# Turning two chunks of scaled keys with one 128x128 transpose, and 32-token products on the column quarters for the second mixer's diagonal and short block lengths

## The chip, the cores and the metric

One core of one Trainium2 chip runs one inference step of a small recurrent decoder. The metric is the time of one execution on the device, in microseconds; lower is better. All arithmetic is in 32-bit floats. TensorE has two lanes in the profile: PE (the matmuls) and PEld (the loads of the stationary operand, which overlap them). A matmul on plain f32 operands leaves two records, since it runs in two passes; one on operands of type fp32r leaves one.

## The reference

Two layers over 512 prompt tokens and 8 samples of 4 tokens (544 columns in all). Layer 0 runs two recurrent mixers side by side (RG-LRU and RWKV-7), layer 1 one (HGRN2), each followed by a gated feed-forward block. Of these, two places matter here. In RWKV-7 a 64x64 matrix state per head is updated by every token:

```python
S = (S * w_t[:, :, None, :] - sk[..., None] * (kk_t * a_t)[:, :, None, :]
     + v_t[..., None] * k_t[:, :, None, :])
return S, jnp.einsum('bhvk,bhk->bhv', S, r_t)
```

In HGRN2 token t attends to every earlier token s with a weight that holds, per channel, the product of all decays between them:

```python
diff = bc[:, :, :, None, :] - bc[:, :, None, :, :]
dec = jnp.exp(jnp.where(mask, diff, -jnp.inf))
att = jnp.einsum('bhtsk,bhtk,bhsk->bhts', dec, qc, kc)
```

## The kernel before

Everything is held with channels on the 128 partitions and the 544 tokens along the free axis. The dense layers are 128x128 weight tiles against 272-token halves. Each weight is split into a high and a low fp32r part (`wh` on ScalarE, `wl` on VectorE or GpSimd, L210 and L213), and three products per tile (high by high, high by low, low by high) accumulate in PSUM tiles named `acc`. Nearly all matmuls are issued through one helper, `mm`, so they carry the line L179; they are told apart by their tiles.

**First mixer (`mixer0`).** RWKV-7 runs in chunks of 64 tokens, two heads on the 128 partitions, four pairs p of heads. Four things are prepared before the scan over chunks. `scores` makes masked products. `keys(p, w)` (L708 to L728) scales the keys by the decay of their chunk (`KH`, on GpSimd, in two buffers) and turns them so that tokens stand on the partitions (`TM`): `turn` multiplies each 64x64 block by an identity, two per chunk and sixteen per call into one PSUM tile `tmps`, and one ScalarE copy of 128x512 takes that to `TM`. A 64-column piece for the samples (`KHs`, L723) is turned behind it when w is 1. A triangular inverse in 32x32 blocks is made by a chain of VectorE steps, `Pd` and `Y` (L683, L685), which starts when `Ns` has been gathered from DRAM and ends in a store (`y_p`) and sixteen loads of the tile `T` (L698). `join` (tiles `jps`) puts the blocks together with 32x32 matmuls. The string `MID` gives the order of these pieces. From the piece `r3` on, the order of TensorE is the order of the code; that of the other engines is set by a scheduler.

**Second mixer (`mixer1`).** HGRN2 works head by head (8 heads) in `mix`. The 512 prompt tokens are four chunks of 128. The attention matrix `A` of a chunk (tokens s on the partitions, t along the free axis) is built from a diagonal and seven levels with block lengths b = 1, 2, 4, ... 64. Before level b, `K` and `Q` have been multiplied by the decays within blocks of b tokens (GpSimd for `K`, L1567; VectorE for `Q`, L1568), so that their plain product is right exactly where s stands in an even block and t in the odd block behind it. Each level multiplies 64 tokens s by the 64 tokens t of the chunk's odd blocks, eight 64x64 products (`lv`) for the four chunks and two halves, though only the pairs in neighbouring blocks are wanted; `copy_predicated` with the mask `lmask` takes these to `A` (L1570). The 32 sample tokens ride along: one 32x32 product `d0s`, and one 32x16 product each at b = 1 and 2. At b = 64 there are four products, one per chunk, copied by ScalarE (L1575). The diagonal (`d0`, in the trace's names `d`) is eight 64x64 products masked by an identity (L1549). In this stage TensorE also runs in the order of the code: behind each level, `fill(FILL[l])` issues 27, 13, 13, 24, 10, 23 and 5 matmuls of the next head's projections, during which `K` and `Q` are brought to the next level.

Of the kernel before, what the change touches and what calls it, by code (L numbers as in the profile page):

```python
# [11 lines left out]
F32 = mybir.dt.float32  # L12
F32R = mybir.dt.float32r
I32 = mybir.dt.int32
# [16 lines left out]
CH = 64  # L31
# [54 lines left out]
def consts_np():  # L86
# [42 lines left out]
    for l in range(7):  # L129
        b = 1 << l  # L130
        t = np.array([x for x in range(128) if (x // b) % 2])[None, :]
        lv.append(((s // b) + 1 == t // b).astype(np.int32))
    c["lmask"] = np.stack(lv, 1)
    return {k: np.ascontiguousarray(v) for k, v in c.items()}


class Build:
# [205 lines left out]
    def mixer0(self):  # L343
# [359 lines left out]
        def turn(out, src):  # L703
            for par in range(2):
                r = par_rows[par]
                self.mm(out[r], src[r], ident[r, r])

        def keys(p, w):  # L708
# [7 lines left out]
            yield  # L716
            ps = self.ms.tile([128, NCH, CH], F32, tag="m", name="tmps")
            for c in range(NCH):
                turn(ps[:, c], KH[:, c])
            ACT(TM[p][:, w], ps, AF.Copy)  # L720
            if w:
# [695 lines left out]
    def mixer1(self, xg):  # L1417
# [5 lines left out]
        p = self.open("m1")  # L1423
        lmask = p.tile([128, 7, 64], I32, name="lmask")
        nc.sync.dma_start(lmask, I["lmask"])
# [5 lines left out]
        for i in range(2):  # L1431
            nc.gpsimd.memset(Am[i][64:128, :, 0:64], 0.0)
        qms = [p.tile([128, NB, 32], F32, name=f"qm{i}") for i in range(2)]
# [20 lines left out]
        def tmp(name, shape=None, bufs=2):  # L1454
            return p.tile(shape or [128, NT], F32, tag=name, name=name, bufs=bufs)

        def blk(z, b, n):
            return z[:, 0:n].rearrange("p (m g b) -> p m g b", g=2, b=b)
# [77 lines left out]
        def mix(h, late):  # L1536
# [4 lines left out]
            As = tmp("As", [32, 32])  # L1541
            ps = self.ms.tile([128, 4, 64], F32, tag="m", name="d0")
            for c in range(4):
                for g in range(2):
                    ks = slice(128 * c + 64 * g, 128 * c + 64 * g + 64)
                    self.mm(ps[64 * g:64 * g + 64, c], K[:, ks], q0[:, ks])
            for g in range(2):
                r = slice(64 * g, 64 * g + 64)
                TT(A[r, :, r], ps[r], self.ident[r, None, r].to_broadcast([64, 4, 64]), OP.mult)  # L1549
            ps = self.ms.tile([32, 32], F32, tag="m", name="d0s")  # L1550
            self.mm(ps, K[:, SEQ:], q0[:, SEQ:])
            TT(As, ps, self.ident[0:32, 0:32], OP.mult)
            for l in range(7):
                b = 1 << l
                ps = self.ms.tile([128, 5, 64], F32, tag="m", name="lv")
                for c in range(4):
                    for g in range(2 if b < 64 else 1):
                        ks = slice(128 * c + 64 * g, 128 * c + 64 * g + 64)
                        self.mm(ps[64 * g:64 * g + 64, c], K[:, ks],
                                blk(Q[:, 128 * c:128 * c + 128], b, 128)[:, :, 1])  # L1560
                if b <= 2:
# [6 lines left out]
                TT(qv[:, :, 1], qv[:, :, 1], g2[:, :, 0, None].to_broadcast([128, m, b]), OP.mult)  # L1568
                if b < 64:
                    nc.vector.copy_predicated(  # L1570
                        A.rearrange("p c (m g b) -> p c m g b", g=2, b=b)[:, :, :, 1],
                        lmask[:, l, None, :].to_broadcast([128, 4, 64]).rearrange("p c (m b) -> p c m b", b=b),
                        ps[:, 0:4].rearrange("p c (m b) -> p c m b", b=b))
                else:
                    ACT(A[0:64, :, 64:], ps[0:64, 0:4], AF.Copy)  # L1575
                if b <= 2:
                    nc.vector.copy_predicated(
                        blk(As, b, 32)[:, :, 1], lmask[0:32, l, 0:16].rearrange("p (m b) -> p m b", b=b),
                        ps[0:32, 4, 0:16].rearrange("p (m b) -> p m b", b=b))
# [198 lines left out]
```

## Time and profile before

| | |
|---|---|
| median of 3 runs | 1546.02 us (1541.61, 1546.02, 1546.65) |
| the profiled execution | 1542.56 us, span 1540.8 us, mean granted clock 0.981 |
| PE busy | 1480.7 us of the span |
| VectorE (DVE) busy | 831.7 us |
| ScalarE (ACT) busy | 549.4 us |
| GpSimd (POOL) busy | 401.9 us |
| `mixer1`, from the first `d0` product to the last level | 809 to 1060 us of the span |
| first turned keys to the last | 106 to 168 us of the span |

A row of the timeline gives the start, the length, the engine, the line, the operation with its tiles and its shape, and how many instructions were merged; brackets give the idle time before it and what ended it. The length of a merged row runs from the first start to the last end, so the last instruction's own duration is in it. A shape such as 128\*64 128x64 means that 128 rows and 64 columns of the array were used and that the moving operand had 128 partitions and 64 elements.

### The profile page before, as it was taken

To read this page: it belongs to the slowest core of one execution; us is meant where nothing else is said; L and a number is where in the kernel's file an instruction comes from. 1 tells how busy PE (TensorE), PEld (TensorE's weight loads), DVE (VectorE), ACT (ScalarE), POOL (GpSimd) and SP (SyncE) were. 2 spreads that over 40 slices of the span, in tenths; PEclk is the share of its full clock that TensorE was granted. 3 is DMA by queue.
4 is the path that set the end of the run, shared out by engine and by line. 5 is a ranking of instruction groups with operands and counts; after the bars stand their busy time and mean duration, and the time that the engine had idled before them with its cause. 6 is when DMAs were issued, how large, how long until landed. Compare 5 with 4: busy or idle time off the path is not lost.

```text
span 1540.8 us, 34923 instructions
## 1 busy us (share of the span) xinstructions
PE 1480.7 (96%) x14688; PEld 1432.2 (93%) x14688; DVE 831.7 (54%) x1542; ACT 549.4 (36%) x983; POOL 401.9 (26%) x520
## 2 busy tenths in 40 slices
PE   7988899879999999999999999999999999999998
PEld 6877898669999999999999999999999999999997
DVE  6776346655544444434576666666674433443444
ACT  4642144453432233223352333333453322232224
POOL 3583245422110011001123434444431100110010
PEclk9999999879999999999999999999999999999999
DMA  4222221132232322322231222322333223223221
GB/s 159 70 71 85 59 80 41 43 97 76 83 90 89 87 92 83 91 88 88 82 121 63 86 95 85 104 92 87 101 122 92 90 83 90 90 90 90 84 75 59
DMA packets 87405, 132.89 MB, mean 86 GB/s; under 512 B 24368, under 2 KB 30384, under 8 KB 87120
## 3 DMA queue, kind: packets, MB, share of 16 engines
q1 hardware_dynamic: 87248, 130.66, 27.4%
q8 instruction: 115, 1.88, 0.5%
q14 instruction: 42, 0.34, 0.1%
HBM read 120.13 MB, written 10.50 MB: 85 GB/s over the span
## 4 chain that ended last, share of the span: by engine, by line
PE 85%; DVE 6%; ACT 3%; DMA 2%; issue 2%; POOL 1%; SPq 1%; DVEq 0%; ACTq 0%; POOLq 0%
PE acc L179 74%; PE lv L179 2%; PE ops L179 2%; PE ch L179 1%; PE jps L179 1%; SPq L698 1%; DMA wf<-w_out_ab 1%; PE ds L179 0%; PE tr L1593 0%; PE nps L179 0%; DVE Y L685 0%; DVE wl L213 0%; ACT wh L210 0%; DMA wd<-down 0%; PE opsm L179 0%
## 5 line engine op out<-in xcount | busy, mean ns | idle before, releaser
L179 PE MATMUL acc<-xg,wh 128*128 128x272 f32 x4544 | 877.2, 291 | 12.6 <-ACT xg L270 6.2
L179 PEld LDWEIGHTS acc<-xg,wh 128*128 128x128 f32 x4544 | 717.1, 190 | 20.5 <-ACT xg L270 6.5
L179 PE MATMUL acc<-xg,wl 128*128 128x272 f32 x2272 | 651.6, 292 | 0.1
L210 ACT ACTIVATE wh<-wf 128x512 fp32r<-128x512 f32 (+1 forms) x404 | 250.9, 621 | 630.2 <-PE acc L179 521.8
L179 PEld LDWEIGHTS acc<-xg,wl 128*128 128x128 f32 x2272 | 427.0, 190 | 4.5 <-issue 0.8
L213 DVE TENSOR_TENSOR wl<-wf,wh 128x512 fp32r<-128x512 f32 (+1 forms) x373 | 267.2, 717 | 188.9 <-ACT wh L210 163.0
L1297 POOL TENSOR_TENSOR S<-S,rstd 128x272 f32<-128x272 f32 x88 | 74.7, 849 | 645.5 <-ACT S L1296 645.4
L179 PE MATMUL acc<-h,wh 128*128 128x272 f32 x1280 | 236.9, 288 | 0.0
L179 PEld LDWEIGHTS acc<-h,wh 128*128 128x128 f32 x1280 | 198.0, 188 | 0.0
L179 PE MATMUL acc<-h,wl 128*128 128x272 f32 x640 | 176.7, 287 | 0.0
L179 PEld LDWEIGHTS acc<-h,wl 128*128 128x128 f32 x640 | 118.1, 188 | 0.0
L1300 DVE TENSOR_TENSOR hh<-acc,S 128x272 f32<-128x272 f32 x88 | 38.9, 441 | 126.2 <-PE acc L179 124.7
L179 PE MATMUL acc<-cat,wh 128*128 128x272 f32 (+2 forms) x512 | 99.5, 294 | 7.3 <-ACT wh L210 7.3
L179 PEld LDWEIGHTS acc<-cat,wh 128*128 128x128 f32 x512 | 81.8, 192 | 8.2 <-ACT wh L210 7.8
L1296 ACT ACTIVATE S<-t 128x272 f32<-128x272 f32 x88 | 37.8, 431 | 122.2 <-DVE t L1295 122.2
L1317 DVE TENSOR_TENSOR x<-acc,x 128x272 f32<-128x272 f32 x80 | 35.0, 439 | 81.3 <-PE acc L179 81.0
L179 PE MATMUL acc<-cat,wl 128*128 128x272 f32 (+2 forms) x256 | 73.6, 295 | 3.4 <-POOL wl L213 3.1
L1295 DVE TENSOR_TENSOR t<-acc,rstd 128x272 f32<-128x272 f32 x88 | 38.7, 441 | 70.1 <-PE acc L179 70.1
L288 POOL TENSOR_TENSOR ssq<-ssq,sq 128x544 f32<-128x544 f32 x33 | 46.6, 1411 | 87.6 <-ACT sq L287 84.9
L1567 POOL TENSOR_TENSOR K<-K,G 128x256 f32<-128x256 f32 (+1 forms) x48 | 39.2, 817 | 78.5 <-PE lv L179 78.5
L213 POOL TENSOR_TENSOR wl<-wf,wh 128x512 fp32r<-128x512 f32 x31 | 41.5, 1343 | 65.7 <-ACT wh L210 65.5
L179 PEld LDWEIGHTS acc<-cat,wl 128*128 128x128 f32 x256 | 48.6, 192 | 4.4 <-POOL wl L213 3.6
(368 smaller groups left out, 1560.0 us busy)
## 6 DMA issues: line engine op xcount, KB each, us to landing
wf<-gate SPq DMA_DIRECT2D x88, 256.0 KB, 2.7
wf<-up SPq DMA_DIRECT2D x88, 256.0 KB, 2.8
wf<-down SPq DMA_DIRECT2D x72, 256.0 KB, 2.7
wf<-w_in_c SPq DMA_DIRECT2D x64, 256.0 KB, 2.6
wf<-w_in_ab SPq DMA_DIRECT2D x44, 256.0 KB, 2.8
x<-xT SPq DMA_DIRECT2D x16, 272.0 KB, 4.8
wf<-w_out_ab SPq DMA_DIRECT2D x16, 256.0 KB, 2.6
S<-hS SPq DMA_DIRECT2D x8, 512.0 KB, 3.6
```

Of the source, the lines that this page charges most:

```text
L179: return self.seq(self.nc.tensor.matmul(out, lhsT, rhs, start=start, stop=stop, skip_group_check=True), chain)
L210: nc.scalar.activation(wh[:, :n], wf[:, :n], AF.Copy)
L213: eng.tensor_tensor(wl[:, :n], wf[:, :n], wh[:, :n].bitcast(F32), OP.subtract)
L288: eng.tensor_tensor(self.ssq, self.ssq, t, OP.add)
L698: nc.sync.dma_start(T[quarter(par, half), :, p, CB * half:CB * half + CB], y_p[2 * p + par, half::2].rearrange("c i t -> i c t"))
L1295: nc.vector.tensor_tensor(t[:, c], ps, rs()[:, c], OP.mult)
L1296: nc.scalar.activation(S[:, c], t[:, c], AF.Silu)
L1297: nc.gpsimd.tensor_tensor(S[:, c], S[:, c], rs()[:, c], OP.mult)
L1300: nc.vector.tensor_tensor(hh[:, c], ps, S[:, c], OP.mult)
L1317: nc.vector.tensor_tensor(x[:, c], ps, x[:, c], OP.add)
L1567: PTT(kv[:, :, 0], kv[:, :, 0], g2[:, :, 1, None].to_broadcast([128, m, b]), OP.mult)
```

## The change

Three edits. First, `keys` turns two chunks at a time: a block of 128 partitions (two heads) by 128 tokens (two chunks) goes through one transpose, four per call instead of sixteen products; since its result has the tokens of the two chunks on the two halves of the partitions and the heads along the free axis, four ScalarE copies of 64 partitions by 256 elements sort it into `TM`. Second, the diagonal and the levels b = 1 to 16 of `mixer1` use products of 32 tokens s, at the four 32-column groups of the array and so on the four 32-partition quarters of PSUM: sixteen products with 32 columns for the diagonal, sixteen with the 16 odd-block tokens of the same quarter for a level. They land in a compact tile `Ad` (128 by 4 by 32); at b = 16 four GpSimd copies spread it into `A`. Third, b = 32 is eight 32x32 products (quarter 0 against 1, quarter 2 against 3), copied by two ScalarE instructions. The mask shrinks, and `A` is now zeroed whole.

```diff
-            ps = self.ms.tile([128, NCH, CH], F32, tag="m", name="tmps")
-            for c in range(NCH):
-                turn(ps[:, c], KH[:, c])
-            ACT(TM[p][:, w], ps, AF.Copy)
+            ps = self.ms.tile([128, 4, 128], F32, tag="m", name="tmps")
+            for c in range(4):
+                self.seq(nc.tensor.transpose(ps[:, c], KH[:, 2 * c:2 * c + 2].rearrange("p c t -> p (c t)"), ident))
+            for odd in range(2):
+                for par in range(2):
+                    ACT(TM[p][par_rows[par], w, odd::2], ps[par_rows[odd], :, par_rows[par]], AF.Copy)
...
-            nc.gpsimd.memset(Am[i][64:128, :, 0:64], 0.0)
+            nc.gpsimd.memset(Am[i], 0.0)
...
-            ps = self.ms.tile([128, 4, 64], F32, tag="m", name="d0")
+            quads = [slice(32 * q, 32 * q + 32) for q in range(4)]
+            ps = self.ms.tile([128, 4, 32], F32, tag="m", name="d0")
             for c in range(4):
-                for g in range(2):
-                    ks = slice(128 * c + 64 * g, 128 * c + 64 * g + 64)
-                    self.mm(ps[64 * g:64 * g + 64, c], K[:, ks], q0[:, ks])
-            for g in range(2):
-                r = slice(64 * g, 64 * g + 64)
-                TT(A[r, :, r], ps[r], self.ident[r, None, r].to_broadcast([64, 4, 64]), OP.mult)
+                for r in quads:
+                    ks = slice(128 * c + r.start, 128 * c + r.stop)
+                    self.mm(ps[r, c], K[:, ks], q0[:, ks])
+            Ad = tmp("Ad", [128, 4, 32])
+            TT(Ad, ps, sum4[:, None, :].to_broadcast([128, 4, 32]), OP.mult)
...
                 for c in range(4):
-                    for g in range(2 if b < 64 else 1):
-                        ks = slice(128 * c + 64 * g, 128 * c + 64 * g + 64)
-                        self.mm(ps[64 * g:64 * g + 64, c], K[:, ks],
-                                blk(Q[:, 128 * c:128 * c + 128], b, 128)[:, :, 1])
+                    Kc, Qc = K[:, 128 * c:128 * c + 128], Q[:, 128 * c:128 * c + 128]
+                    if b < 32:
+                        for r in quads:
+                            self.mm(ps[r, c, 0:16], Kc[:, r], blk(Qc[:, r], b, 32)[:, :, 1])
+                    elif b == 32:
+                        for r, t in ((quads[0], quads[1]), (quads[2], quads[3])):
+                            self.mm(ps[r, c, 0:32], Kc[:, r], Qc[:, t])
+                    else:
+                        self.mm(ps[0:64, c], Kc[:, 0:64], Qc[:, 64:128])
...
-                if b < 64:
+                if b < 32:
                     nc.vector.copy_predicated(
-                        A.rearrange("p c (m g b) -> p c m g b", g=2, b=b)[:, :, :, 1],
-                        lmask[:, l, None, :].to_broadcast([128, 4, 64]).rearrange("p c (m b) -> p c m b", b=b),
-                        ps[:, 0:4].rearrange("p c (m b) -> p c m b", b=b))
+                        Ad.rearrange("p c (m g b) -> p c m g b", g=2, b=b)[:, :, :, 1],
+                        lmask[:, l, None, :].to_broadcast([128, 4, 16]).rearrange("p c (m b) -> p c m b", b=b),
+                        ps[:, 0:4, 0:16].rearrange("p c (m b) -> p c m b", b=b))
+                elif b == 32:
+                    for r, t in ((quads[0], quads[1]), (quads[2], quads[3])):
+                        ACT(A[r, :, t], ps[r, 0:4, 0:32], AF.Copy)
                 else:
                     ACT(A[0:64, :, 64:], ps[0:64, 0:4], AF.Copy)
+                if b == 16:
+                    for r in quads:
+                        nc.gpsimd.tensor_copy(A[r, :, r], Ad[r])
```

On TensorE nothing changes its place; only the counts and shapes of these products do. At the start of a head in `mixer1` the program of before has these rows on that engine (`d` is the diagonal, `d0s` the samples' product, `lv` level b = 1, `acc` the projections that fill):

```order
L179 MATMUL d_10039<-q_9958,K 64x64 x8
L179 MATMUL d0s<-q_9958,K 32x32
L179 MATMUL lv<-Q,K 64x64 x8
L179 MATMUL lv<-Q,K 32x16
L179 MATMUL acc<-xg,wh 128x272 x2
```

The changed program has these at the same place:

```order
L179 MATMUL d_9967<-q_9886,K 32x32 x16
L179 MATMUL d0s<-q_9886,K 32x32
L179 MATMUL lv<-Q,K 32x16 x17
L179 MATMUL acc<-xg,wh 128x272 x2
L179 MATMUL acc<-xg,wl 128x272
```

Sixteen smaller products stand for eight, and the samples' 32x16 product now has the shape of its neighbours.

On GpSimd, from the `K` update of b = 16 to that of b = 64 in the first head, before (`G` are decay products of the next head's projection):

```order
L1567 TENSOR_TENSOR K<-K,G 128x16x16
L1493 TENSOR_TENSOR G<-G 128x8
L1493 TENSOR_TENSOR G<-G 128x4
L1567 TENSOR_TENSOR K<-K,G 128x8x32
L1567 TENSOR_TENSOR K<-K,G 128x4x64
```

and in the changed program:

```order
L1574 TENSOR_TENSOR K<-K,G 128x16x16
L1495 TENSOR_TENSOR G<-G 128x16
L1588 COPY A_9708<-Ad 32x4x32 x4
L1495 TENSOR_TENSOR G<-G 128x8
L1574 TENSOR_TENSOR K<-K,G 128x8x32
L1495 TENSOR_TENSOR G<-G 128x4
L1574 TENSOR_TENSOR K<-K,G 128x4x64
```

The four copies, which wait for VectorE's last masked copy into `Ad`, stand ahead of the `K` update of b = 32.

In `mixer0` the scheduler moves GpSimd's work around the second pair of keys (`KH` and `KHs` are the scaled keys, `d` the difference of neighbouring tokens for the next projection, `Ws` a piece of the scores' input):

```order
 L487 TENSOR_TENSOR d<-X 128x544
-L710 TENSOR_TENSOR KH<-KB_248,ebT 128x512
-L488 TENSOR_TENSOR d<-shift,X 128x8
-L710 TENSOR_TENSOR KH<-KB_248,ebT 128x512
+L710 TENSOR_TENSOR KH<-KB_248,ebT 128x512 x2
 L713 TENSOR_TENSOR KHs<-KBs_260,ebT 128x64
-L745 TENSOR_TENSOR Ws_254<-rm,eb_292 64x32
-L745 TENSOR_TENSOR Ws_258<-rm,eb_292 64x32
-L478 MEMSET X 128x1
+L488 TENSOR_TENSOR d<-shift,X 128x8
 L710 TENSOR_TENSOR KH<-KB_249,ebT 128x512
```

The small `d` of L488 now stands behind both scalings and `KHs` instead of between them, and a third scaling comes ahead of `Ws`.

More of the change, by code (lines that the diff above doesn't have):

```diff
@@ L132, in consts_np @@
         lv.append(((s // b) + 1 == t // b).astype(np.int32))
-    c["lmask"] = np.stack(lv, 1)
+    c["lmask"] = np.ascontiguousarray(np.tile(np.stack(lv, 1)[0:32, 0:5, 0:16], (4, 1, 1)))
     return {k: np.ascontiguousarray(v) for k, v in c.items()}
@@ L1423, in mixer1 @@
         p = self.open("m1")
-        lmask = p.tile([128, 7, 64], I32, name="lmask")
+        lmask = p.tile([128, 5, 16], I32, name="lmask")
         nc.sync.dma_start(lmask, I["lmask"])
```

## The prediction

> **What bounds the kernel now.** I read the page's totals first, then the shares of the chain of waits, then the windows of the two stages that the change touches.
>
> ```profile
> span 1540.8 us, 34923 instructions
> PE 1480.7 (96%) x14688; PEld 1432.2 (93%) x14688; DVE 831.7 (54%) x1542; ACT 549.4 (36%) x983; POOL 401.9 (26%) x520
> PE 85%; DVE 6%; ACT 3%; DMA 2%; issue 2%; POOL 1%; SPq 1%; DVEq 0%; ACTq 0%; POOLq 0%
> ```
>
> TensorE is busy in 96% of the span and holds 85% of the chain that ended last; no other engine comes near. Next the stretch of `mixer1` in which the diagonals and levels lie, and one of `mixer0` (per engine: busy us and instructions; then granted clock and DMA).
>
> ```profile
> core 0: us, PE busy (x) PEld busy (x) DVE busy (x) ACT busy (x) POOL busy (x), PEclk, DMA share, GB/s
> 800.00:1070.00 270.00, 269.89 (x2817) 251.31 (x2815) 185.87 (x370) 91.18 (x180) 113.93 (x147) 1.00 0.26 85
> 140.00:150.00 10.00, 7.88 (x303) 6.85 (x300) 4.39 (x11) 1.20 (x2) 0.65 (x4) 0.83 0.43 110
> ```
>
> In `mixer1` TensorE has no gap (269.89 of 270.00) at full clock, and its order is that of the code, so time taken from its products there comes off the end one for one while nothing else is late. In `mixer0` it has gaps, and there the chain has to be read step by step.
>
> **The change, part one: the diagonal and the levels in `mixer1`.** These rows are the second and third head's, from product to the filling `acc` behind it. A plain f32 product leaves two records.
>
> ```profile
> 869.13 0.69 PE L179 MATMUL d<-q,K 128*64 128x64 f32 x16
> 869.92 0.85 PE L179 MATMUL lv<-Q,K 128*64 128x64 f32 x18
> 870.71 0.51 PE L179 MATMUL acc<-xg,wh 128*128 128x272 f32 x2
> 844.24 0.85 PE L179 MATMUL lv<-Q,K 128*64 128x64 f32 x18
> 845.03 0.52 PE L179 MATMUL acc<-xg,wh 128*128 128x272 f32 x2
> 846.85 0.69 PE L179 MATMUL lv<-Q,K 128*64 128x64 f32 x16
> 847.47 0.39 PE L179 MATMUL acc<-xg,wh 128*128 128x272 f32 x1
> 855.17 0.69 PE L179 MATMUL lv<-Q,K 128*64 128x64 f32 x16
> 855.79 0.52 PE L179 MATMUL acc<-xg,wh 128*128 128x272 f32 x2
> ```
>
> From start to the next `acc`, the diagonal with `d0s` and b = 1 takes 870.71 - 869.13 = 1.58 us, b = 2 takes 0.79, b = 4 takes 0.62 (8 and 16 have its shape), b = 32 takes 0.62. Per head that is 1.58 + 0.79 + 3 x 0.62 + 0.62 = 4.85 us. The four products of b = 64 stay.
>
> No row before shows a full-height product of 32 columns with 16 moving elements. The nearest are these: 32x32 tiles with 16 moving elements on four places of the array (`jp`, `jz`), with 32 elements on two places (`jg`, `ja`), and full-height products of 32 columns in four column groups, but with 128 moving elements (`opsq`).
>
> ```profile
> 150.34 1.26 PE L179 MATMUL jps<-jp,jz 32*32 32x16 f32 x128
> 151.53 0.52 PE L179 MATMUL acc<-xg,wh 128*128 128x272 f32 x2
> L179 PE MATMUL jps<-jp,jz 32*32 32x16 f32 x256 | 2.5, 180 | 0.0
> 168.91 1.38 PE L179 MATMUL jps<-jg,ja 32*32 32x32 f32 x64
> 836.43 0.65 PE L179 MATMUL opsq<-S,qm 128*32 128x128 f32 x16
> L179 PE MATMUL opsq<-S,qm 128*32 128x128 f32 x128 | 5.2, 279 | 0.0
> ```
>
> Taking the last record's own duration out, the spacing is (1.26 - 0.18)/127 = 8.5 ns for the first, (1.38 - 0.2)/63 = 18.7 ns for the second (its 0.2 is my estimate, after the first's 180 ns), and (0.65 - 0.279)/15 = 24.7 ns for the third. From the last record's start to the `acc` behind it, 151.53 - (151.60 - 0.18) = 0.11 us pass. I take 8.5 ns for the products on four quarters: the last row shows that four column groups of full height do run side by side (four records of 279 ns in 4 x 24.7 = 99 ns), and its stream is eight times as long as the new one, so the price lies toward the row that shares the length of 16. For b = 32, on two quarters only, I take 18.7. Both ends, 8.5 and 24.7, stay for the range.
>
> - Diagonal, `d0s`, b = 1: 68 records, 67 x 8.5 + 0.11 and 0.05 for the samples' products, which have no neighbour to share the array with: 0.73, so -0.85 us.
> - b = 2: 34 records, 33 x 8.5 + 0.11 = 0.39, so -0.40.
> - b = 4, 8, 16: 32 records, 31 x 8.5 + 0.11 = 0.37, so -0.25 each, -0.75.
> - b = 32: 16 records, 15 x 18.7 + 0.11 = 0.39, so -0.23.
>
> That is 2.23 us a head, and **17.8 us for eight heads**. It all goes to the time if the updates between levels stay covered. Each level's update of `K` and `Q` begins when the level ends and has the filling products beside it, whose number does not change; a shorter level moves both alike.
>
> What is new there stands on GpSimd and ScalarE. Four copies, 32 partitions by 128 elements, follow VectorE's last masked copy at b = 16.
>
> ```profile
> L1004 POOL COPY am<-Ws 64x32 f32<-64x32 f32 x16 | 3.8, 238 | 10.5 <-PE opss L179 5.8 <-PE rpss L179 4.2
> L617 POOL COPY Ws<-kap 64x8 f32<-64x8 f32 x8 | 3.4, 429 | 0.3
> 853.88 0.88 POOL L1567 TENSOR_TENSOR K<-K,G 128x256 f32<-128x256 f32 x1 [0.34 <-PE lv L179]
> 855.95 0.67 POOL L1567 TENSOR_TENSOR K<-K,G 128x256 f32<-128x256 f32 x1 [0.75 <-PE lv L179]
> 858.85 0.68 PE L179 MATMUL lv<-Q,K 128*64 128x64 f32 x8
> L1575 ACT ACTIVATE A<-lv 64x256 f32<-64x256 f32 x8 | 3.0, 378 | 9.7 <-PE lv L179 9.7
> ```
>
> GpSimd copies cost 238 to 429 ns here, so four are 1.0 to 1.7 us. The order puts them behind the `K` update that ends at 853.88 + 0.88 = 854.76, with one `G` product of about 0.24 between, and ahead of the update that b = 64 waits for: that would end by 854.76 + 0.24 + 1.7 + 0.67 = 857.4 at the latest. b = 64 starts at 858.85, less 0.23 of its own head's b = 32: 858.6. About 1.2 us is left, so I count them at nothing; if that cover went, each us would cost 8 us in all. ScalarE's two copies at b = 32 (378 ns or less each) feed nothing until the end of the head. VectorE's masked copies shrink from 256 elements to 64; that engine is not late there. The smaller mask and the whole memset come once, ahead of the stage: nothing.
>
> **Part two: the turned keys in `mixer0`.** Rows for a 128x128 transpose and for sixteen products by the identity (32 records), then steps of the chain of waits:
>
> ```profile
> 860.42 0.60 PE L1593 MATMUL tr<-ident,V 128*128 128x128 f32 x4
> 860.85 0.60 PE L1593 MATMUL tr<-ident,K 128*128 128x128 f32 x4
> 135.99 1.15 PE L179 MATMUL tmps<-ident,KH 64*64 64x64 f32 x32
> 143.52 1.90 DMA T<-y_p
> 163.78 0.55 PE tmps L179 x13
> 164.32 1.72 issue
> 166.04 0.80 PE tmps L179 x19
> 166.87 0.60 ACT L720 ACTIVATE TM<-tmps 128x512 f32<-128x512 f32 x1 [2.68 <-PE tmps L179]
> ```
>
> Four transposes take 860.85 - 860.42 = 0.43 us against 1.15 (1.35 without the stall for the last call, 0.55 + 0.80). There are eight calls; those before 143 lie in front of the wait for the loads of `T`, which end at 143.52 + 1.90 = 145.42, and win nothing. Only the last call's stand on the chain: 0.43 - 1.35 = -0.9 us, with the 1.72 of `issue`, whose cause no row names, left in. ScalarE makes four copies for one; at most four times 0.60 instead of 0.60, with 2.68 us idle ahead of it. Only a consumer straight behind the last call would see 1.8 us of that.
>
> Against this stands the order. `d` of L488 moves behind `KH` and `KHs`, and VectorE's `rm` waits for it:
>
> ```profile
> 109.40 0.22 POOL L488 TENSOR_TENSOR d<-shift,X 128x8 f32<-128x8 f32 x1
> 109.66 0.78 DVE L489 SCALAR_TENSOR_TENSOR rm<-d,vec,X 128x544 f32<-128x544 f32 x1 [4.34 <-POOL d L488]
> 110.04 1.30 POOL L710 TENSOR_TENSOR KH<-KB,ebT 128x512 f32<-128x512 f32 x1 [0.42 <-PE tmps L179]
> 111.30 0.74 POOL L713 TENSOR_TENSOR KHs<-KBs,ebT 128x64 f32<-128x64 f32 x1
> ```
>
> `rm` comes later by up to 1.30 + 0.74 - 0.42 = 1.6 us. VectorE's queue then holds the triangular chain, which ends in the store and loads of `T`; since `rm` comes once ahead of that chain, and VectorE has waited 4.34 us for it, I put about half, +0.7, on the loads of `T`. Together **-0.2 us**, with bounds of -3 (-0.9 and the whole stall of 1.72 gone with the burst, `rm` hidden: -2.6) and +3 (`rm` and the ScalarE copies whole, 1.6 + 1.8 - 0.9 = 2.5).
>
> **Sum.** On the profiled execution: 1542.56 - 17.8 - 0.2 = 1524.6 us. The median of the runs, 1546.02, lies 3.46 above that execution, which gives 1528.0 on its basis. I predict 1528.
>
> **The rivals.** A measurement of this kernel tells about 0.3%, 4.6 us, from no change.
>
> *The small products cannot start faster than the full-height row shows.* Then 24.7 ns holds for all 67 + 33 + 93 + 15 = 208 intervals of a head: 208 x 24.7 + 0.71 (the tails) = 5.85 us against 4.85, so +1.0 a head and +8.0 in all: 1550.4 on the profile's basis, 1554 on the median's, slower. It decides from (4.85 - 0.71)/208 = 19.9 ns up. For it: the only full-height row has 24.7, and the record count of a level doubles. Against it: that row's stream is long, and `jp`, `jz` shows 8.5 from the same queue with as many weight loads. The Trainium skill ("TensorE: Matmul & The Clock Gate", section "Wait — 56ns, not 53.3ns?") says that start-to-start never drops below about 25 ns however small the product, which is this rival; the 8.5 ns of tiles that share the array contradict it for 32 rows, and no run here shows it for 128 rows. "Instruction Overhead" in the Trainium skill's "TensorEngine Tiling (Array Packing)" warns against tiling a dimension that is already small, on the same ground.
>
> *Only two of the four column groups run together*, as the row at 18.7 ns: 208 x 18.7 + 0.71 = 4.60, -0.25 a head, -2.0 in all: 1540.4, or 1543.8 on the median's basis; no change that can be told. `opsq` speaks against it.
>
> *GpSimd's copies hold b = 64 back.* If a copy took 0.7 us or more, 2.8 for four, the 1.2 us left would be overrun by a little; at 0.95 each by about 1 us a head, and the time would be 1536. Their price of 429 ns for 8 elements speaks for caution.
>
> *`mixer0` gives back its upper bound*: +3 instead of -0.2, 1531.
>
> **How the numbers follow.** The forecast with `mixer0` anywhere in its bounds has 0.78; the copies 0.08; two groups 0.08; the 25 ns floor 0.06. The first two are faster by over 0.3%, the third is the same, the last slower: 0.86, 0.08, 0.06. The forecast's own bounds are 1528 - 3 - some 3 for a mean spacing of 7 ns (208 x 1.5 ns x 8 = 2.5), 1521, and upward 1531 to 1536 by the two rivals that stay faster; 1540 leaves out the third and the last.
>
> **What would show it.** In the profile after, `lv` rows of 32 records with the next `acc` 0.37 us behind their start, and 0.73 from the first `d` to `acc`; rows at 0.9 would be the floor. TensorE still without a gap from 800 on, and no wait for `K` or a copy ahead of b = 64. In `mixer0`, four transposes in 0.43 us, the end of `T`'s loads against 145.42, and the stall near 164. The prediction is wrong if the spacing lies above 12 ns, or if TensorE waits anywhere in `mixer1`.

## The result, and the profile after

| | before | changed |
|---|---|---|
| median of 4 runs | 1545.05 us | 1523.46 us (1521.26 to 1527.63) |
| ratio | | 0.9866, 95% interval 0.9838 to 0.9894 |
| profiled execution | 1542.56 us, span 1540.8 | 1527.63 us, span 1525.6 |

The change makes the kernel faster by 21.6 us on the medians; 1528 was predicted, with its bounds at 1521 and 1540. The profiled execution is the longest of the four, so stages are compared below, not spans.

First the totals and the chain of waits of the changed kernel, as on the page:

```profile
span 1525.6 us, 36071 instructions
PE 1466.0 (96%) x15232; PEld 1419.6 (93%) x15232; DVE 807.9 (53%) x1526; ACT 561.1 (37%) x1023; POOL 415.7 (27%) x552
PE 86%; DVE 5%; issue 3%; ACT 2%; POOL 2%; DMA 2%; SPq 0%; DVEq 0%; POOLq 0%; ACTq 0%
```

TensorE has 544 more records and 14.7 us less busy time, and still bounds the kernel. The windows of the two stages:

```profile
core 0: us, PE busy (x) PEld busy (x) DVE busy (x) ACT busy (x) POOL busy (x), PEclk, DMA share, GB/s
800.00:1070.00 270.00, 269.59 (x3712) 253.91 (x3711) 174.00 (x369) 104.15 (x212) 133.82 (x183) 1.00 0.27 93
140.00:150.00 10.00, 7.77 (x210) 5.89 (x210) 2.76 (x6) 0.00 (x0) 0.57 (x3) 0.63 0.37 74
150.00:160.00 10.00, 8.54 (x208) 7.51 (x209) 2.20 (x5) 1.95 (x4) 0.00 (x0) 0.69 0.08 29
```

`mixer1` has stayed without a gap worth counting. In `mixer0`, at the joins, the granted clock is lower than before (0.63 against 0.83 at 140 to 150).

**Where the time went.** The rows of one tile give the first and last start of its instructions. From the first head's diagonal `d` to the last `opsm`, which forms the last head's output, the kernel before and then the changed one:

```profile
L179 PE MATMUL d<-q,K x128: 222/222/270, 809.1 to 1039.2; 128*64 128x64 f32 x128
L179 PE MATMUL opsm<-sum,Oi x16: 276/286/297, 838.5 to 1070.3; 128*128 128x32 f32 x16
L179 PE MATMUL d<-q,K x256: 195/196/218, 810.7 to 1026.2; 128*32 128x32 f32 x128
L179 PE MATMUL opsm<-sum,Oi x16: 275/286/298, 838.0 to 1055.2; 128*128 128x32 f32 x16
```

That stage took 1070.3 - 809.1 = 261.2 us and takes 1055.2 - 810.7 = 244.5: 16.7 us less, 2.09 a head. What follows it is the same to 0.1 us (1540.8 - 1070.3 = 470.5, 1525.6 - 1055.2 = 470.4). What precedes it ends 1.6 us later in these two executions, though the medians say the opposite: 21.6 - 16.7 = 4.9 us must be won there. So the runs below are read by two numbers each: this stage, from the profile, and the rest ahead of it, the median less the time from the first `d` to the end of the span (before: 1545.05 - 731.7 = 813.4; changed: 1523.46 - 714.9 = 808.6; 2 us outside of the span are in it).

The levels of the second head after the change, from products to the `acc` behind them:

```profile
838.39 0.46 PE L179 MATMUL d<-q,K 128*32 128x32 f32 x32
839.15 0.51 PE L179 MATMUL acc<-xg,wh 128*128 128x272 f32 x2
842.94 0.49 PE L179 MATMUL lv<-Q,K 128*32 128x16 f32 x34
843.36 0.52 PE L179 MATMUL acc<-xg,wh 128*128 128x272 f32 x2
845.19 0.45 PE L179 MATMUL lv<-Q,K 128*32 128x16 f32 x32
845.56 0.39 PE L179 MATMUL acc<-xg,wh 128*128 128x272 f32 x1
852.79 0.45 PE L179 MATMUL lv<-Q,K 128*32 128x32 f32 x16
853.16 0.52 PE L179 MATMUL acc<-xg,wh 128*128 128x272 f32 x2
```

Diagonal to b = 1 takes 0.76 us (0.73 was predicted), b = 2 takes 0.42 (0.39), b = 4 takes 0.37 (0.37), b = 32 takes 0.37 (0.39).

### The profile page after: what moved, and what is told of

It is laid out like the page before. It is cut to its first block, busy times and chain, and to the rows that moved or that the text cites. A ratio compares the mean times of both kernels' runs of the same rounds, so it can differ in the third digit from the quotient of the medians.

```text
span 1525.6 us, 36071 instructions
## 1 busy us (share of the span) xinstructions
PE 1466.0 (96%) x15232; PEld 1419.6 (93%) x15232; DVE 807.9 (53%) x1526; ACT 561.1 (37%) x1023; POOL 415.7 (27%) x552
## 3 DMA queue, kind: packets, MB, share of 16 engines
q8 instruction: 119, 1.95, 0.5%
## 4 chain that ended last, share of the span: by engine, by line
PE 86%; DVE 5%; issue 3%; ACT 2%; POOL 2%; DMA 2%; SPq 0%; DVEq 0%; POOLq 0%; ACTq 0%
PE acc L179 77%; PE ops L179 2%; PE lv L179 2%; PE ch L179 1%; DMA wf<-w_out_ab 1%; PE nps L179 1%; POOL wl L213 1%; PE jps L179 0%; PE ds L179 0%; PE tr L1606 0%; POOL KH L710 0%; PE opsm L179 0%; PE gps L179 0%; PE rpss L179 0%; ACT wh L210 0%
```

## The experiments

All times in one table; each kernel was timed beside the kernel before on its chip. "Stage" and "ahead" are the two numbers explained above. "Turned" says which keys go through the 128x128 transpose.

| kernel | turned | median, us | ratio to before, interval | stage | ahead |
|---|---|---|---|---|---|
| before | none | 1545.05 | | 261.2 | 813.4 |
| the change | all | 1523.46 | 0.9866, 0.9838 to 0.9894 | 244.5 | 808.6 |
| levels_only | none | 1530.63 | 0.9906, 0.9887 to 0.9925 | 244.4 | 815.6 |
| keys_only | all | 1543.28 | 0.9986, 0.9973 to 1.0000 | 261.2 | 811.3 |
| change_again | all | 1521.87 | 0.9859, 0.9837 to 0.9881 | 244.5 | 806.9 |
| four_groups | all | 1520.61 | 0.9850, 0.9830 to 0.9871 | 241.7 | 808.7 |
| by_quarter | all | 1542.77 | 0.9986, 0.9974 to 0.9998 | 263.3 | 809.2 |
| half_stream | none | 1543.80 | 0.9993, 0.9975 to 1.0010 | 260.2 | 813.4 |
| copies_8 (and a shorter group norm) | all | 1529.10 | 0.9892, 0.9876 to 0.9908 | 247.7 | 811.1 |
| keep_warm | all | 1523.26 | 0.9855, 0.9838 to 0.9871 | 244.4 | 808.1 |
| last_keys | last pair | 1524.34 | 0.9851, 0.9830 to 0.9872 | 244.4 | 809.7 |
| first_keys | all but last pair | 1523.73 | 0.9856, 0.9834 to 0.9879 | 244.5 | 807.9 |
| pad_j | all | 1519.34 | 0.9839, 0.9820 to 0.9858 | 241.9 | 807.3 |
| best | last pair | 1522.94 | 0.9851, 0.9831 to 0.9871 | 241.8 | 810.3 |

The stage repeats to 0.2 us wherever the levels are the same; "ahead" carries all the scatter.

The granted clock is a good part of why. In all fourteen traces it is either 1.0 or 0.5, and every stretch at 0.5 lies in the first 362 us or in the last 9, none in the stage. To take this out I multiplied each run's span by its mean granted clock, which is on record for every run. That is an estimate of the time at full clock, and it flatters a kernel whose clock is low while TensorE waits anyway. Over the 52 runs of the kernel before, the span and the part of it lost to the clock (span times one less the clock) go together with a correlation of 0.70, which is half of the scatter; the mean at full clock is 1512.2 us.

### The two halves of the change apart

`levels_only` keeps the second and third edit and turns keys as before:

```diff
+            ps = self.ms.tile([128, NCH, CH], F32, tag="m", name="tmps")
+            for c in range(NCH):
+                turn(ps[:, c], KH[:, c])
+            ACT(TM[p][:, w], ps, AF.Copy)
```

> The diagonal and levels of the change, with the keys turned as before. Theory 1 (the levels carry the gain): from the first diagonal product to the last output sum of mixer1 the stage is 14.6 us shorter over seven heads as in the profile of the change (2.09 a head), so about 16.7 us below the kernel before, ratio near 0.989. Theory 2 (the turned keys carry part of the measured 21.6 us): this kernel stays 3 to 6 us behind the whole change.

`keys_only` is the kernel before with the first edit alone (the lines of `keys` in the diff above).

> Only the turned keys, the second mixer as before. Theory 1: within 3 us of the kernel before, with rm and so the loads of T about 2 us later, as in the profile of the change, and 0.9 us won at the last call. Theory 2 (the keys carry part of the gain): 3 to 6 us faster than before.

`change_again` is the change, unaltered.

> The change itself once more beside its parts. If the parts add up, its gain is that of the levels alone plus that of the keys alone to within 2 us. Theory 1: 16 to 18 us below before; theory 2: 20 to 22.

The stage falls by 16.8 us with the levels alone and by nothing with the keys alone, so that half is settled. In the runs, the levels alone win 0.94% (14.5 us, interval 11.6 to 17.5) and the keys alone 0.14% (2.2 us, 0 to 4.2); the whole wins 1.41% (21.8 us) on the same chip. The last is 5 us more than the sum of the parts (14.5 + 2.2), which the intervals only just allow. Of theory 2's figures only that of the whole came out (20 to 22): the levels alone stay 7 to 9 us behind the whole change by the medians, not 3 to 6, and the keys alone win less than 3. At full clock, by the estimate above, the parts do add: on that chip the means of the runs fall by 17.7 us with the levels, 7.0 with the keys and 25.4 with both.

### Why a small product is cheap

`by_quarter` issues the same products quarter by quarter, so that neighbours in the queue share a column group:

```diff
-            for c in range(4):
-                for r in quads:
+            for r in quads:
+                for c in range(4):
...
+                if b < 32:
+                    for r in quads:
+                        for c in range(4):
+                            Kc, Qc = K[:, 128 * c:128 * c + 128], Q[:, 128 * c:128 * c + 128]
+                            self.mm(ps[r, c, 0:16], Kc[:, r], blk(Qc[:, r], b, 32)[:, :, 1])
...
-                        for r in quads:
-                            self.mm(ps[r, c, 0:16], Kc[:, r], blk(Qc[:, r], b, 32)[:, :, 1])
+                        pass
```

> The change with the diagonal and b = 1 to 16 issued quarter by quarter (four chunks of one column group behind each other) instead of chunk by chunk. Same products, same count. If the gain comes from four column groups that work side by side, neighbours in the queue now share a group and run one behind the other: a level of 32 records takes 0.8 to 1.0 us instead of 0.37, about +3 us a head, 20 to 28 us in all. If the products are only limited by how fast they can be issued (about 8 ns a record), nothing changes.

Its timeline, level b = 4 of the second head:

```profile
844.72 0.89 PE L179 MATMUL lv<-Q,K 128*32 128x16 f32 x32
845.54 0.39 PE L179 MATMUL acc<-xg,wh 128*128 128x272 f32 x1
```

The level takes 0.82 us instead of 0.37 and the stage 263.3 us instead of 244.5, 18.8 more (20 to 28 were expected); with that the second mixer is slower than before the change. Same products, same count, another order. The spacing is (0.82 - 0.11)/31 = 22.9 ns within a group, and (0.37 - 0.11)/31 = 8.4 ns over four. A quarter of 22.9 would be 5.7, so over four groups something else sets the pace, and no run shows what. The floor that the Trainium skill states ("TensorE: Matmul & The Clock Gate", section "Wait — 56ns, not 53.3ns?", start-to-start never below about 25 ns) is thus about right here for one column group, by these 22.9 ns, and not for products that alternate between four.

`half_stream` keeps 64-token products in two groups and halves only what streams through them:

```diff
-                        self.mm(ps[64 * g:64 * g + 64, c], K[:, ks],
-                                blk(Q[:, 128 * c:128 * c + 128], b, 128)[:, :, 1])
+                        if b < 64:
+                            self.mm(ps[64 * g:64 * g + 64, c, 32 * g:32 * g + 32], K[:, ks],
+                                    blk(Q[:, ks], b, 64)[:, :, 1])
+                        else:
+                            self.mm(ps[0:64, c], K[:, ks], Q[:, 128 * c + 64:128 * c + 128])
...
+                    for g in range(2):
+                        r, s = slice(64 * g, 64 * g + 64), slice(32 * g, 32 * g + 32)
+                        nc.vector.copy_predicated(
+                            A[r, :, r].rearrange("p c (m g b) -> p c m g b", g=2, b=b)[:, :, :, 1],
+                            lmask[r, l, None, s].to_broadcast([64, 4, 32]).rearrange("p c (m b) -> p c m b", b=b),
+                            ps[r, 0:4, s].rearrange("p c (m b) -> p c m b", b=b))
```

> The kernel before (64-token products, two column groups), but each level below 64 multiplies only by the 32 odd-block tokens of its own 64-token half, and VectorE copies each half apart. Keys as before. If a product's streaming time in its group sets the pace, a level falls to 16 records at about 15 ns, 0.35 us, as in the change with its 32 records, and the levels win about 1.3 us a head, 10 to 11 us in all, without any quarter. If the four quarters are what wins, a level stays at 0.5 us or more and the gain is under 6 us.

Its level b = 4:

```profile
848.83 0.66 PE L179 MATMUL lv<-Q,K 128*64 128x32 f32 x16
849.42 0.39 PE L179 MATMUL acc<-xg,wh 128*128 128x272 f32 x1
```

0.59 us against 0.62 before: half the stream wins 0.03 us, and 1.0 us in the whole stage. The first theory is wrong for products of 64 columns. With the last record's own duration taken out (0.22 us in its group, 0.20 in that of `d`), a record takes (0.66 - 0.22)/15 = 29 ns with 64 columns and 32 moving elements; the diagonal of the change, also with 32 moving elements but 32 columns, takes (0.46 - 0.20)/31 = 8.4 ns. So at the same stream the price depends on the columns of a product and the number of groups in turn. That half the stream wins next to nothing here is in line with the Trainium skill's "TensorEngine Tiling (Array Packing)", section "Instruction Overhead", that a product with one moving element takes as long as one with 60; its warning against tiling what is small already does not hold here, since the four groups overlap.

A long stream does count: over the same four groups a record of 32 columns takes 24.7 ns with 128 elements (`opsq`), and 8.4 with 32 or with 16.

`four_groups` takes the same thought further. Odd chunks of b = 32 land one quarter higher and odd chunks of b = 64 on the upper half:

```diff
-                        for r, t in ((quads[0], quads[1]), (quads[2], quads[3])):
-                            self.mm(ps[r, c, 0:32], Kc[:, r], Qc[:, t])
+                        for q in (0, 2):
+                            self.mm(ps[quads[q + c % 2], c, 0:32], Kc[:, quads[q]], Qc[:, quads[q + 1]])
                     else:
-                        self.mm(ps[0:64, c], Kc[:, 0:64], Qc[:, 64:128])
+                        self.mm(ps[64 * (c % 2):64 * (c % 2) + 64, c], Kc[:, 0:64], Qc[:, 64:128])
...
+                    for q in (0, 2):
+                        for z in range(2):
+                            ACT(A[quads[q], z::2, quads[q + 1]], ps[quads[q + z], z:4:2, 0:32], AF.Copy)
...
+                    for z in range(2):
+                        ACT(A[0:64, z::2, 64:], ps[64 * z:64 * z + 64, z:4:2], AF.Copy)
```

> The change, with b = 32 spread over all four column groups (odd chunks land one quarter higher) and b = 64 over two halves, six ScalarE copies instead of three. If spacing is set by how many column groups work side by side: b = 32 falls from about 0.39 to 0.25 us and b = 64 from about 0.6 to 0.37, 0.3 to 0.4 us a head and 2.5 to 3 us in all below the change. If a floor per product or the weight loads set it: no difference.

Its second head, b = 32 and b = 64:

```profile
852.40 0.33 PE L179 MATMUL lv<-Q,K 128*32 128x32 f32 x16
852.66 0.52 PE L179 MATMUL acc<-xg,wh 128*128 128x272 f32 x2
855.72 0.45 PE L179 MATMUL lv<-Q,K 128*64 128x64 f32 x8
856.10 0.39 PE L179 MATMUL acc<-xg,wl 128*128 128x272 f32 x1
```

b = 32 takes 0.26 us (0.37 in the change) and b = 64 takes 0.38 (0.61 in the change). The stage is 2.8 us shorter, as expected of groups that work side by side.

### The cover on GpSimd

`copies_8` makes each copy of the diagonal block twice. It differs in a second place, which its expectation does not name: the group norm of `mixer0` makes two refinement steps instead of three, three small VectorE instructions fewer each time. That lies ahead of the stage, so only the stage of this kernel is read, and not its time:

```diff
-            for _ in range(3):
+            for _ in range(2):
                 TT(w, y, y, OP.mult)
...
                     for r in quads:
-                        nc.gpsimd.tensor_copy(A[r, :, r], Ad[r])
+                        for _ in range(2):
+                            nc.gpsimd.tensor_copy(A[r, :, r], Ad[r])
```

> The change with each GpSimd copy of the diagonal block made twice, eight instead of four a head. In the profile of the change the four took 1.82 us and the K update behind them ended at 855.20, 1.02 us ahead of b = 64. If that slack is all the cover there is, 1.8 us more overruns it by 0.8 us a head: +6 us, with TensorE waiting for K ahead of b = 64. If GpSimd is far off the path: no change.

The change's GpSimd in the second head, and TensorE's b = 64:

```profile
852.51 1.82 POOL L1588 COPY A<-Ad 32x128 f32<-32x128 f32 x4
854.58 0.62 POOL L1574 TENSOR_TENSOR K<-K,G 128x256 f32<-128x256 f32 x1
856.22 0.68 PE L179 MATMUL lv<-Q,K 128*64 128x64 f32 x8
```

`K` is ready at 854.58 + 0.62 = 855.20, 1.02 us ahead of its level. In `copies_8` the scheduler put three of the added copies behind that update and ahead of the next one, which the transposes of `K` wait for:

```profile
828.19 2.13 POOL L1589 COPY A<-Ad 32x128 f32<-32x128 f32 x3
830.61 0.61 POOL L1574 TENSOR_TENSOR K<-K,G 128x256 f32<-128x256 f32 x1
831.28 0.66 PE L1607 MATMUL tr<-ident,K 128*128 128x128 f32 x4 [0.47 <-POOL K L1574]
```

The weight loads of these transposes wait 3.3 us for `K` in all, in seven of the eight heads, and the stage is 3.2 us longer: half of the 6 expected, and at another place than expected. So the copies of the change are covered, and doubling them is not.

### The clock at the joins

`keep_warm` fills TensorE's wait for `T` with 24 large products ahead of the first join, whose result nobody reads:

```diff
+            if e == "j" and not warm:
+                warm = True
+                ps = self.ms.tile([128, 4, 128], F32, tag="m", name="warm")
+                for i in range(24):
+                    self.mm(ps[:, i % 4], ident, ident)
```

> The change with 24 products of the identity by itself (128x128, result unread) ahead of the first join, while TensorE waits for the loads of T. In the profile of the change the granted clock is 0.63 at 140 to 150 and 0.69 at 150 to 160 us, against 0.83 and 1.00 before the change. Theory C (the idle wait lowers the clock and the joins behind it run slowly): the clock from 145 to 160 returns to about 1.0, the first join products end earlier, 3 to 5 us below the change. Rival (the path there runs through DMA and VectorE): no gain, or a loss of up to 5 us of added products.

The windows of the change, and then of `keep_warm`:

```profile
145.00:150.00 5.00, 4.37 (x170) 3.56 (x170) 0.00 (x0) 0.00 (x0) 0.00 (x0) 0.50 0.34 82
150.00:155.00 5.00, 3.54 (x54) 2.70 (x54) 0.93 (x2) 1.20 (x2) 0.00 (x0) 0.50 0.02 6
```

```profile
145.00:150.00 5.00, 2.71 (x174) 2.38 (x168) 0.00 (x0) 0.00 (x0) 0.00 (x0) 0.93 0.38 85
150.00:155.00 5.00, 5.00 (x237) 4.39 (x229) 1.55 (x4) 1.19 (x2) 0.00 (x0) 0.72 0.17 59
139.26 5.62 PE L179 MATMUL warm<-ident 128*128 128x128 f32 x48
148.40 0.23 PE L179 MATMUL jps<-T,NTt 32*32 32x16 f32 x2 [2.02 <-DMA T<-y_p]
```

The clock did come back (0.50 to 0.93, then 0.72), but a join still waited 2.02 us for a load of `T`, until 148.40 (in the change the last such wait ends at 147.56), and the time is that of the change. The rival is right: filling the wait wins nothing, since the loads of `T` end it.

### Which of the turned keys win

`last_keys` turns only the last pair by transposes, `first_keys` all but the last pair:

```diff
+            if p == 0:
                 ps = self.ms.tile([128, 4, 128], F32, tag="m", name="tmps")
...
+            else:
+                ps = self.ms.tile([128, NCH, CH], F32, tag="m", name="tmps")
+                for c in range(NCH):
+                    turn(ps[:, c], KH[:, c])
+                ACT(TM[p][:, w], ps, AF.Copy)
```

(`p != 0` in the other.)

> The change, but only the last pair of heads (its two calls, the last ones ahead of the scan) is turned by 128x128 transposes; the first six calls are turned as before. VectorE, GpSimd and the output projection then keep the order that they have with the keys turned as before. Theory P (the keys win on TensorE where the last calls stand on the chain): the gain of the keys over the levels alone (1530.6 in the run of that kernel, about 4.6 us by the medians of all kernels so far) stays whole or grows to 6, since T is not late: 1524 to 1526. Theory S (they win because the scheduler puts VectorE's and ScalarE's work in another order, in the output projection among it): no gain, 1529 to 1531.

> The counterpart: the first six calls by transposes, the last pair as before; the order on VectorE, GpSimd and in the output projection is that of the change. Theory P: the last call costs its 0.9 us and the stall again and T stays late: 1529 to 1533. Theory S: 1522 to 1525, as the whole change.

By their medians both come out at the time of the whole change, so each theory is half refuted: the last pair alone gives a gain without any reordering, and the others alone give one without the last pair. The two gains don't add.

### Stalls that nothing releases

The chain of before has 1.72 us of `issue` in the last call; the changed kernel has such stalls elsewhere. I numbered TensorE's instructions by start in each trace (products, weight loads and the few of its sequencer) and looked up the number of every stall over half a us without a releaser between 147 and 215 us:

```
before        3266 (1.25 us)   3778 (1.72)   4802 (1.49)
levels_only   3778 (1.66)   4802 (2.06)   5570 (2.37)
half_stream   3778 (1.34)   4802 (1.53)   5570 (1.47)
the change    2498 (1.56)   4290 (2.29)   4802 (1.12)
change_again  2498 (1.73)   4290 (2.32)   4802 (1.23)
keys_only     2498 (1.21)   4290 (2.16)   4802 (2.11)
four_groups   2498 (1.18)   4290 (2.34)   4802 (1.56)
by_quarter    2498 (1.50)   4290 (2.31)   4802 (1.49)
copies_8      2498 (1.41)   4290 (2.29)   4802 (1.01)
keep_warm     4290 (1.76)
last_keys     4546 (2.21)
best          4546 (2.38)
first_keys    4290 (2.06)
pad_j         4290 (2.08)
```

Every number is 194 above a multiple of 256. `pad_j` tests it. It is `four_groups` with 96 more small instructions ahead of the first join:

```diff
+            if e == "j" and not pad:
+                pad = True
+                ps = self.ms.tile([128, 4, 128], F32, tag="m", name="pad")
+                for i in range(24):
+                    r = slice(32 * (i % 4), 32 * (i % 4) + 32)
+                    self.mm(ps[r, 0, 0:16], ident[r, r], ident[r, r][:, 0:16])
```

> The version with b = 32 and 64 spread, plus 24 tiny products (32x16, result unread, 96 TensorE instructions counting weight loads) ahead of the first join, where TensorE waits for T anyway; no other engine's order moves. In all profiles so far TensorE's stalls of 1 to 2.4 us without a releaser among the dense 32x32 and 64x64 products stand at instruction numbers that are 194 above a multiple of 256 (2498, 4290, 4802 in the change; 3266, 3778, 4802, 5570 before), whatever the code there. Theory F (fetching of instructions in blocks of 256): they stay at such numbers although the code has moved by 96, and as in the kernel with 24 large products only one or two of three remain; 1.5 to 3 us faster than the 1520.6 of the version without them. Rival (they belong to the code): the stalls move along by 96 to 2594, 4386, 4898 and the time stays.

The rows of `four_groups` with its two later stalls, and of `pad_j` with its only one:

```profile
189.59 0.26 PE L179 MATMUL jps<-ident,T 32*32 32x32 f32 x1 [2.34 <-issue]
200.41 0.21 PE L179 MATMUL ops<-U,KB 64*64 64x64 f32 x1 [1.56 <-issue]
```

```profile
187.61 0.26 PE L179 MATMUL jps<-T,NTt 32*32 32x16 f32 x3 [2.08 <-issue]
```

The stall stays at number 4290 although other code stands there (a product of `T` and `NTt` in place of one of the identity and `T`); those at 2498 and 4802 are gone, and none stands at 2594, 4386 or 4898. So they belong to the place in the instruction stream. The time is 1519.3 against 1520.6, less than the 1.5 to 3 expected and within the scatter.

`best` joins `last_keys` and `four_groups`, to see whether a version without the reordering profits more:

> The last pair's keys by transposes, the other six calls as before, with b = 32 and b = 64 spread over the column groups. Theory (the gains add): 3.0 us less than the 1524.3 of the same kernel without the spread levels, the stage of mixer1 241.5 us from the first diagonal to the last output sum against 244.5, 1521 in all, no better than the change with spread levels (1520.6). If a run comes out below 1518, the two halves of the keys' change hinder each other.

It is 1522.94, the stage 241.8 as expected. It does not beat `four_groups` or `pad_j`. The fastest kernels here are these two, whose intervals overlap with the change's; what is sure of their gain is the stage, 2.6 to 2.8 us.

## Why the prediction was right, point by point

- **The bound.** TensorE without a gap in `mixer1`, so that products taken away come off the end: shown. The stage gave 16.7 us where 17.8 were forecast. By the quoted head, 0.76 + 0.42 + 3 x 0.37 + 0.37 = 2.66 us against 4.85 before, 2.19 a head and 17.5 in all; but the rows are rounded. Added up in the traces over all diagonals and levels of the eight heads, from first product to the `acc` behind, it is 43.3 us before and 26.5 after, 16.8 in all. The forecast was about 1 us too large by that rounding and by the samples' products, which cost 0.03 us more than counted at each of b = 1 and 2. By the prediction's own sign TensorE should wait nowhere in `mixer1`; it waits twice 0.2 us for `Q`, which it did not before, once here:

```profile
913.83 0.44 PE L179 MATMUL lv<-Q,K 128*32 128x16 f32 x32 [0.20 <-DVE Q L1575]
```

- **The price of 8.5 ns** (8.4 measured), chosen between 8.5 and 24.7, was right, and so was its reason as far as the runs go. That groups in turn run side by side is what `by_quarter` shows. That the long stream of `opsq` is what makes it dear fits too: over the same four groups 128 elements cost 24.7 ns, and 32 or 16 cost 8.4. What was not foreseen is that below 32 elements the stream buys nothing more; in products of 64 columns, as in `half_stream`, even the step from 64 to 32 won next to nothing. The 18.7 for b = 32 came out as (0.45 - 0.20)/15 = 16.7. One statement was wrong: the kernel before does have full-height products of 32 columns and 16 elements, those of the samples at b = 1 and 2, but each stands alone, so no spacing could have been read from them.
- **The rivals.** The floor of some 25 ns exists, at 22.9 ns, within one column group; the order chunk by chunk avoids it, and the same products in the other order would have cost 18.8 us, and the gain. Two groups only: excluded by the same numbers.
- **The lower bound.** 1528 - 3 - 3 is 1522, where the prediction has 1521; the two medians of the change, 1523.46 and 1521.87, lie about there.
- **GpSimd's copies.** Predicted 1.0 to 1.7 us for four and 1.2 us left; measured 1.82 us and 1.02 left, and `copies_8` shows how near the edge that is. (Copies of 0.7 us would still have fitted by the prediction's own figures: 2.8 - 1.7 = 1.1 us more, where 1.2 was left.)
- **The turned keys** are the term that was mis-sized: "-0.2 us, with bounds of -3 and +3". Five kernels with all keys turned and nothing else altered ahead of the stage (the change twice, `keys_only`, `four_groups`, `by_quarter`) have 806.9 to 811.3 us there, mean 808.9; three with the keys as before have 813.4, 813.4 and 815.6, mean 814.1. That is -5.2 us, beyond the bound; `keys_only` beside the kernel before on its own chip, -2.2 (0 to -4.2), is within it. Both of its steps were there, in other sizes. The last call's four transposes:

```profile
167.42 0.66 PE L719 MATMUL tmps<-ident,KH 128*128 128x128 f32 x4
167.92 0.27 PE L725 MATMUL tmps<-ident,KHs 128*64 128x128 f32 x1
```

They take 167.92 - 167.42 = 0.50 us, and the stall of 1.72 is not among them: 2.6 us less than the call of before, where -0.9 was counted and -2.6 kept as a bound. But the stall is moved and not won: between 147 and 215 us the kernel before has three such stalls of 4.5 us in all, the change three of 5.0. That leaves 1.35 - 0.50 = 0.85 us, the -0.9 that was counted. Against it, `T` is later by more than the 0.7 us that was put on it. The triangular chain's first step on VectorE, before and after, and the store behind its last one:

```profile
113.30 1.05 DVE L683 TENSOR_TENSOR Pd<-Y,Ns 128x30 f32<-128x30 f32 x1
L692 SPq DMA_DIRECT2D y_p<-Y x1: 320/320/320, 131.9 to 131.9; - x1
```

```profile
110.77 1.55 DVE L489 SCALAR_TENSOR_TENSOR rm<-d,vec,X 128x544 f32<-128x544 f32 x1 [5.55 <-POOL d L488]
115.75 0.44 DVE L481 TENSOR_TENSOR X<-acc,rstd 128x272 f32<-128x272 f32 x1 [1.48 <-PE acc L179]
116.11 0.20 DVE L683 TENSOR_TENSOR Pd<-Y,Ns 128x30 f32<-128x30 f32 x1
L692 SPq DMA_DIRECT2D y_p<-Y x1: 320/320/320, 134.3 to 134.3; - x1
```

`rm` is 1.1 us later behind `d`, and an `X` that the prediction didn't count now stands ahead of the chain and waits 1.48 us for TensorE; the chain starts 2.8 us later and its store goes out 2.4 us later. So these two steps, -0.9 us at the last call and `T` 2.4 us later, do not explain a gain of 5 us.

**What stays open.** Where the keys' gain ahead of the stage comes from. That it is there is surer than the medians tell: at full clock, by the estimate above and less the stage, `levels_only` and `half_stream` are 0.5 and 0.6 us below the kernel before, the seven kernels with all keys turned (`copies_8` left out) 6.3 to 8.5, `first_keys` 7.5, and `last_keys` and `best` 4.7 and 5.0. `keep_warm`, whose clock is nearly full in the wait for `T`, is 6.7 below, so the low clock in that wait accounts for at most some 2 us of it. A part lies behind the turned keys: with half of every stretch at 0.5 taken off, the time from the last join to the first `d` is 588.5 to 588.9 us in the three traces with the keys as before and 584.8 to 588.2 in those seven. What in the order of the other engines does that is not shown. Nor do the stalls explain it: `last_keys` and `first_keys` have one of about 2.1 us where the change has three, but `pad_j`, which has one stall too, won only 1.3 us by it. One execution of each kernel was traced, and as measured the start of the stage scatters by as much as the effect (804.6 to 811.5 us with all keys turned by transposes).

## What to carry to other kernels

Products of 32 columns are cheap only in turn: with neighbours in the queue on different column groups they started every 8 ns, with neighbours on the same one every 23, so the order of the loops decides more than the sizes. Where small results can land on any quarter of PSUM, spread them (`four_groups`), and let the copy that is needed anyway put them right. And compare by a stage that repeats: here two timestamps in the profile agreed to 0.2 us where the runs scatter by several, and half of that scatter goes with the granted clock.

## What was not expected of the hardware

TensorE stalls at fixed places of its instruction stream. In all kernels shown, stalls of 1.0 to 2.4 us among dense small products stand 256 instructions or a multiple of it apart, whatever code stands there. The instruction queue of the page, packets and megabytes, fits that:

```profile
q8 instruction: 119, 1.95, 0.5%
```

1.95 MB in 119 packets are 16.4 KB each, 64 bytes for each of 256 instructions. The Trainium skill ("Runtime: NRT & Kernel Launch", section "Terms") says that an engine's instruction memory is refilled in blocks of 16 KiB, which agrees. The number of packets goes with TensorE's instructions: in each of the fourteen traces it is the sum of PE's and PEld's counts on the page divided by 256 and rounded up (115 for 29376 before, 119 for 30464, 113 for 28928 in `keys_only`).

That TensorE waits for its instructions is then seen in the packets themselves, which the traces hold one by one. Instruction 194 + 256k never starts less than 1.0 us after packet k has landed, at any of some 1650 such places in the fourteen traces. At all 32 stalls of the table packet k had landed 1.0 to 1.5 us before TensorE went on (the 9th ahead of 2498, the 16th ahead of 4290, the 18th ahead of 4802); where it had landed earlier, there is no such stall. Dense small products, it seems, use up their instructions faster than these come; why some kernels have one such stall and others three is open.

The scatter of the runs goes with the granted clock. Of 17 runs of the kernel before on one chip, the shortest (1540.58 us) had a mean of 0.983 and the longest (1548.63) one of 0.977. Their spans, 1538.8 and 1546.8 us, come to 1512.6 and 1511.2 when multiplied by it. The stretches at the low clock are 3.4, 6.8, 10.2, 13.7 or 17.1 us long ahead of the stage, which are steps of 3.4, and all at half the clock.
